# A two-layer decoder trunk: another order of the attention steps, and the embedding product among the output projection's last row blocks

## The chip, the core and the metric

The kernel runs on one core of a Trainium2 chip. The metric is device time in microseconds (us), the median of several executions. The engines' names in the profile are PE (TensorE, matmuls) with PEld (its weight loads), DVE (VectorE), ACT (ScalarE), POOL (GpSimd) and SP (SyncE, which here only issues DMAs). PSUM, where matmuls accumulate, has eight banks of 128 x 512 numbers.

## The reference

One sequence of 512 tokens with 1024 features, all in float32. `h` is the residual stream.

```python
def reference(x, p, ...):
    h = x
    for i in range(2):
        xn = rmsnorm(h, norm_mix[i])
        if i == 0:
            h = h + mixer_a(xn, a_w_in[0], a_norm_v[0], a_w_s[0], a_b_s[0], a_w_out[0])
        else:
            h = h + mixer_b(xn, b_w_q[0], b_sinks[0], b_w_o[0], kblk, vblk)
        h = h + conv_ffn(rmsnorm(h, norm_ffn[i]), f_w_up[i], f_conv_w[i], f_conv_b[i], f_w_down[i])
        h = h + per_layer_embed(h, p[i], norm_ple[i], ple_w_in[i], ple_w_gate[i], ple_b_gate[i])
        if i == 0:
            kblk, vblk = shared_kv(h, norm_kv, w_kv)   # 128-key blocks: the one before, and its own
    return rmsnorm(h, norm_final)

def mixer_b(xn, w_q, sinks, w_o, kblk, vblk):        # 16 heads of 64 in 4 groups, one K/V head a group
    q = (xn @ w_q).reshape(B, nb, BLOCK, N_KV_HEADS, GQA_GROUP, HEAD_DIM)
    scores = einsum('bnikgd,bnjkd->bnkgij', q, kblk) * HEAD_DIM ** -0.5
    scores = scores - slopes * dist                  # ALiBi: slope 2 ** (-(head + 1) / 2)
    scores = where(valid, scores, -inf)              # 0 <= dist < 128
    m = maximum(max(scores), sink)
    e = exp(scores - m)
    probs = e / (sum(e) + exp(sink - m))
    return einsum('bnkgij,bnjkd->bnikgd', probs, vblk).reshape(B, S, 1024) @ w_o

def conv_ffn(xn, w_up, conv_w, conv_b, w_down):      # 2816 hidden features, twice
    c = conv3(xn @ w_up)
    g, u = split(c, 2)
    return (silu(g) * u) @ w_down

def per_layer_embed(h, p_i, g_norm, w_in, w_gate, b_gate):
    return (p_i @ w_in) * sigmoid(rmsnorm(h, g_norm) @ w_gate + b_gate)   # p_i: 512 x 256
```

## The kernel before, in words

**Products.** Every large product is made of three matmuls a tile: each operand is split into a high part (a rounded copy, written by ACT) and a low part (the rest, written by DVE), and high x high, high x low and low x high are added in PSUM (`mm3`, lines 184 to 192; `mm3t` with the operands turned). Features lie on partitions, tokens along the row, so most matmuls are 128 x 128 by 128 x 512. In this document a *block* is one `mm3` over one 128-row slice: three matmuls.

**Weights.** `plan` lists all weight loads in the order of use, in units of up to 128 x 1024. `load` (L133) issues a unit's DMA on SP's queue into one of the raw tiles r0 to r5; during the attention only r0 and r1 are in use, since r2 to r5 hold attention tiles. `pump` (L148) converts a unit: cast `wh` on ACT (L163), subtraction `wl` on DVE (L164), into one of four buffers, or into tiles of its own where the plan names them. The activations p of the embedding go through the same list; their converted tiles take the places m4 and m5 of a pool that the attention uses for `prs` and for the masked copies of the even steps.

**The attention of layer 1** (L671 to L839) has 16 steps, 4 groups of heads by 4 token blocks. A step's work goes through these functions:

- `scores` (L681): 8 matmuls into the two banks `sc`.
- `logits` (L694): on DVE a masked copy (L701, not for the first token block), scale plus ALiBi (L702) and the row minimum `low` (L707); POOL first copies the sink column (L699). For the first token block a second masked copy (L704) follows.
- `exps` (L711): four exponentials on ACT. `weights` (L718): reciprocal on DVE, multiplication of `prs` on POOL (L722).
- `turn` (L724): four PE transposes into the bank `tr`; `turned_hi` (L744, ACT) and `turned_lo` (L750, DVE) split the result, and two masked copies on POOL (L753, `pm`) are made of it.
- `mix` (L756): the value product, four matmuls (two for the first token block) into the bank `pv`, with the key block before as a difference.
- `low_rows` (L773, ACT), `outputs` (L785 DVE, L789 ACT, L790 POOL or, for the last two, DVE): the heads' outputs as high and low tiles `o2`.

`slopes` (L676) makes the ALiBi tile of a group with four POOL products, once a group. `project` makes the queries of the next group, one block at a time; `queries` (L594) splits them (L252, L253) and moves their halves with four DMAs on SP's queue (L602, L603). `merge` makes parts of the output projection into a bank `mm` and adds the sum to `h` on DVE (L669). The loop at L811 runs a software pipeline: in iteration i scores(i), the value product of step i-2, logits(i), one or two of the other blocks, the turning of step i-1, then the rest of the blocks. Between them the iterations carry 6, 5, 5, 5, 5, 5, 5, 4, 4, 4 blocks of queries and then 4, 8, 4, 4, 8, 4 blocks of the first half of the projection. The first half of each row block m is closed and added to `h`; the second half follows in two further iterations and in the loop at L842, where `nf.take(m)` (L285) splits the finished row block for the next norm (ACT L248, DVE L249, square on ACT L277, sum on POOL L282).

**After it** comes the feed-forward part of layer 1 (`ffn`, L346): 22 up products `up(j)` of 16 blocks each, in three parts, each followed by its share of the down product (`dense_add`, L334). Just before the last share stands the layer's embedding product (`ple_in_both`, L407): for half of the tokens with features on partitions (48 matmuls of 256 columns), for the other half with tokens on partitions (24 matmuls of 512 columns), copied out of PSUM by ACT.

**Order.** The framework makes the semaphores, and it arranges each engine's queue by the written order and by what it reckons to be ready; so the trace follows the written order in the main, with some matmuls pulled ahead (in step 1, eleven matmuls of queries stand before the turning where six are written).

Of the kernel before, what the change touches and what calls it, by code (L numbers as in the profile page):

```python
# [52 lines left out]
def tile_yoco(ctx: ExitStack, tc: tile.TileContext, t, out: bass.AP, out_b: bass.AP):  # L53
# [40 lines left out]

    def plan_ffn(l):
        for i, (j0, j1) in enumerate(PARTS):
            if i == 0:
                plan_cols(t["w_up"][l], j1, KD)
            else:
                plan_cols(t["w_up"][l, j0 + 1 : j1], j1 - j0 - 1, KD)  # L100
            if i + 1 < len(PARTS):
                plan_cols(t["w_up"][l, j1 : j1 + 1], 1, KD)
            else:
                plan(t["pT"][l].rearrange("p a b -> p (a b)"), 2 * S, S, own=[(mp, "m4", "m5")])
                plan_cols(t["w_pin"][l], 2, 4)
            plan_cols(t["w_down"][l], 4, j1 - j0, k0=j0)
# [14 lines left out]
    for k0 in (0, 4):  # L121
        plan_cols(t["w_o"], 4, 4, k0=k0)
# [8 lines left out]
    state = {"raw": 0, "unit": 0, "next": 0, "tags": list(range(RAWS)), "turn": 0}  # L131
# [16 lines left out]
    def pump(upto):  # L148
        while state["unit"] < min(upto, len(units)):
# [184 lines left out]
    def dense_add(xs, kk, norm):  # L334

        for c in range(4):
            parts = chunk(256, kk)
            for j in range(2):
                m = 2 * c + j
                ps = psum(f"d{m}")  # L340
                mm3(ps, parts, xs, j * P)
# [4 lines left out]
    def ffn(l, norm, nxt):  # L346
# [35 lines left out]
        for i, (j0, j1) in enumerate(PARTS):  # L382
            act += [up(j) for j in range(j0 + 1, j1)]
            last = j1 == NJ
            if last:
                pe = ple_in_both() if l else ple_in(l)
            nact = [] if last else [up(j1)]
            dense_add(act, j1 - j0, nxt if last else None)
# [18 lines left out]
    def ple_in_both():  # L407

        pw = chunk(S, 2)
        px = [(a[:, o : o + S], b[:, o : o + S]) for a, b, o in pw]  # L410
        first = [(a[:, :N], b[:, :N]) for a, b in px]
        feat, tok = [], []
        for c in range(2):
            parts = chunk(256, 4)
            pf = mp.tile([P, 4, N], F32, tag=f"m{c}", name=f"pef{c}")
            for j in range(4):
                ps = psum(f"pinf{c}_{j}")[:, :N]
                mm3(ps, parts[j // 2 * 2 : j // 2 * 2 + 2], first, j % 2 * P)
                nc.scalar.copy(pf[:, j, :], ps)
                feat.append(pf[:, j, :])  # L420

            wh, wl = (x.rearrange("p (q k n) -> p q k n", q=2, k=2) for x in parts[0][:2])
            for i in range(2):
                if c == 0:
                    tok.append(mp.tile([P, D], F32, tag=f"m{2 + i}", name=f"pet{i}"))
                ps = psum(f"pint{c}_{i}")
                s = slice(N + i * P, N + (i + 1) * P)
                for k, (xh, xl) in enumerate(px):
                    nc.tensor.matmul(ps, xh[:, s], wh[:, :, k, :], start=k == 0, stop=False)
                    nc.tensor.matmul(ps, xl[:, s], wh[:, :, k, :], start=False, stop=False)  # L430
                    nc.tensor.matmul(ps, xh[:, s], wl[:, :, k, :], start=False, stop=k == 1)
                nc.scalar.copy(tok[i][:, c * S : (c + 1) * S], ps)
        return feat, tok
# [226 lines left out]
    def merge(m, k0, k1, first, last, tag="mm"):  # L660
# [4 lines left out]
        if first:  # L665
            box[f"o{m}"] = psum(f"o{m}_{half}", tag)
# [9 lines left out]
    def slopes(g):  # L676

        for e in range(GQ):
            nc.gpsimd.tensor_scalar_mul(alibi[:, e, :], dist, slope(GQ * g + e))
# [13 lines left out]

    def logits(i, o):  # L694
# [4 lines left out]
        nc.gpsimd.tensor_copy(pr[:, :, P], nsink[:, GQ * g : GQ * (g + 1)])  # L699
# [76 lines left out]
    def outputs(i, ps, b):  # L776
# [10 lines left out]
        for a in range(2):  # L787
            oh, ol = o2[2 * g + a]
            nc.scalar.copy(oh[:, cols], of[:, a, :])  # L789
            (nc.gpsimd if i < last - 1 else nc.vector).tensor_sub(ol[:, cols], of[:, a, :], oh[:, cols].bitcast(F32))  # L790

    last = len(steps)
    beside = {i: [] for i in range(last + 2)}
    u = 0
    for i, n in enumerate((6, 5, 5, 5, 5, 5, 5, 4, 4, 4)):
        beside[i] = [(project, u + a) for a in range(n)]
        u += n
    assert u == 48
    for a, ms in enumerate(((0,), (1, 2), (3,), (4,), (5, 6), (7,))):
        beside[10 + a] = [(merge, m, 0, 4, True, True) for m in ms]  # L800
    beside[16] = [(merge, m, 4, 6, True, False) for m in (0, 1)]
    beside[17] = [(merge, 2, 4, 6, True, False), (merge, 3, 4, 6, True, False), (merge, 4, 4, 6, True, False, "tr")]

# [5 lines left out]
    slopes(0)  # L809
    pump(state["next"] + WBUFS)  # L810
    for i in range(last + 2):  # L811
        if i < last:
            o = scores(i)
        if i >= 2:
            pv = mix(i - 2)
        if i < last:
            logits(i, o)
        if i >= 2:
            pb = low_rows(i - 2, pv)
        early = 2 if i < 10 else 1  # L820
        fill(i, 0, early)
        if 0 <= i - 1 < last:
            tr = turn(i - 1)
        if i >= 2:
            outputs(i - 2, pv, pb)
        if i < last:
            exps(i, (0,))
        if 0 <= i - 1 < last:
            turned_hi(i - 1, tr)
        if i < last:  # L830
            exps(i, (1, 2, 3))
        if 0 <= i - 1 < last:
            turned_lo(i - 1, tr)
        fill(i, early, None)
# [215 lines left out]
```

## Time and profile before

| | |
|---|---|
| median of 3 executions | 1153.9 us (1153.18 to 1155.84) |
| the profiled execution | 1154.12 us, of which span 1152.4 us |
| PE busy in the span | 1130.3 us |
| DVE, ACT, POOL busy | 737.9, 508.8, 148.6 us |
| mean granted clock of PE | 0.994 |
| attention steps in the trace | 594 to 698 us |
| last row blocks of the output projection | 698 to 716 us |
| embedding product of layer 1 | 1043 to 1054 us |

The times of the trace count from the start of the span. "Busy" of PE is drawn from modelled ends of pipelined matmuls: one 128 x 512 matmul shows 389 ns, while the next one starts 227 to 230 ns after it. A row of the groups of instructions reads: line, engine, operation, tile written and tiles read, shape, count, then busy us, mean ns of one, and the idle time of the engine before them with what ended it. A row of the waits reads: who waited, for whom, total us, how often, the longest.

### The profile page before, as it was taken

To read this page: it belongs to the slowest core of one execution; us is meant where nothing else is said; L and a number is where in the kernel's file an instruction comes from. 1 tells how busy PE (TensorE), PEld (TensorE's weight loads), DVE (VectorE), ACT (ScalarE), POOL (GpSimd) and SP (SyncE) were. 2 spreads that over 40 slices of the span, in tenths; PEclk is the share of its full clock that TensorE was granted. 3 is DMA by queue.
4 is the path that set the end of the run, shared out by engine and by line. 5 is a ranking of instruction groups with operands and counts; after the bars stand their busy time and mean duration, and the time that the engine had idled before them with its cause. 6 is when DMAs were issued, how large, how long until landed. Compare 5 with 4: busy or idle time off the path is not lost.

```text
span 1152.4 us, 13748 instructions
## 1 busy us (share of the span) xinstructions
PE 1130.3 (98%) x5248; PEld 938.4 (81%) x5248; DVE 737.9 (64%) x984; ACT 508.8 (44%) x811; POOL 148.6 (13%) x181
## 2 busy tenths in 40 slices
PE   9999999999999999999999999999999999999996
PEld 7888888888888888888888777788888888888895
DVE  7356477763676367557868787777636763675656
ACT  6534344431344234544567665444323442445542
POOL 2100310000000000022216654100000000000232
PEclk9999999999999999999999999899999999999998
DMA  9322322332322333232063323323323323333201
GB/s 328 103 89 86 98 94 92 108 98 85 110 83 82 110 122 95 78 114 104 19 175 102 108 74 111 108 78 106 104 80 109 85 81 113 119 100 112 87 18 73
DMA packets 44690, 116.48 MB, mean 101 GB/s; under 512 B 4936, under 2 KB 16848, under 8 KB 44624
## 3 DMA queue, kind: packets, MB, share of 16 engines
q1 hardware_dynamic: 43504, 114.42, 31.4%
q10 hardware_dynamic: 1120, 1.18, 0.3%
q8 instruction: 41, 0.67, 0.2%
q14 instruction: 25, 0.20, 0.1%
HBM read 108.24 MB, written 2.11 MB: 96 GB/s over the span
## 4 chain that ended last, share of the span: by engine, by line
PE 88%; DVE 4%; ACT 3%; POOL 2%; issue 1%; DMA 1%; SPq 0%; POOLq 0%; ACTq 0%; DVEq 0%
PE up L190 14%; PE up L191 14%; PE up L192 14%; PE d L190 8%; PE d L192 8%; PE d L191 8%; PE gate L190 2%; PE gate L192 2%; PE gate L191 2%; PE u L192 1%; PE u L190 1%; PE u L191 1%; PE v L202 1%; PE v L203 1%; PE v L201 1%
## 5 line engine op out<-in xcount | busy, mean ns | idle before, releaser
L164 DVE TENSOR_TENSOR wl<-wraw,wh 128x1024 fp32r<-128x1024 f32 (+2 forms) x197 | 237.9, 1209 | 126.2 <-ACT wh L163 123.6
L163 ACT CAST wh<-wraw 128x1024 fp32r<-128x1024 f32 (+1 forms) x196 | 202.2, 1032 | 239.5 <-PE d L191 133.1
L191 PE MATMUL up<-nf10l,wh 128*128 128x512 f32 x352 | 138.4, 393 | 1.0 <-DVE nf10l L249 1.0
L190 PE MATMUL up<-nf10h,wh 128*128 128x512 f32 x352 | 138.1, 392 | 0.6 <-ACT nf10h L248 0.6
L192 PE MATMUL up<-nf10h,wl 128*128 128x512 f32 x352 | 137.9, 392 | 0.0
L190 PE MATMUL up<-nf00h,wh 128*128 128x512 f32 x352 | 137.1, 390 | 0.0
L192 PE MATMUL up<-nf00h,wl 128*128 128x512 f32 x352 | 137.0, 389 | 0.0
L190 PE MATMUL d<-ah,wh 128*128 128x512 f32 x352 | 136.9, 389 | 0.0
L191 PE MATMUL up<-nf00l,wh 128*128 128x512 f32 x352 | 136.9, 389 | 0.0
L191 PE MATMUL d<-al,wh 128*128 128x512 f32 x352 | 136.9, 389 | 0.0
L192 PE MATMUL d<-ah,wl 128*128 128x512 f32 x352 | 136.9, 389 | 0.0
L368 ACT ACTIVATE c<-hs,vec 128x512 f32<-128x512 f32 x88 | 71.7, 815 | 88.2 <-DVE hs L364 87.5
L369 DVE SCALAR_TENSOR_TENSOR c<-hs,vec,c 128x511 f32<-128x511 f32 x88 | 65.8, 748 | 37.6 <-ACT c L368 37.4
L342 DVE TENSOR_TENSOR h<-h,d 128x512 f32<-128x512 f32 x56 | 38.4, 686 | 73.0 <-PE d L192 73.0
L191 PEld LDWEIGHTS up<-nf10l,wh 128*128 128x128 f32 x352 | 66.7, 190 | 15.4 <-DVE nf10l L249 1.7
L190 PEld LDWEIGHTS up<-nf10h,wh 128*128 128x128 f32 x352 | 66.7, 189 | 14.9 <-ACT nf10h L248 1.1
L192 PEld LDWEIGHTS up<-nf10h,wl 128*128 128x128 f32 x352 | 66.8, 190 | 14.0
L192 PEld LDWEIGHTS up<-nf00h,wl 128*128 128x128 f32 x352 | 66.1, 188 | 13.9
L192 PEld LDWEIGHTS d<-ah,wl 128*128 128x128 f32 x352 | 66.1, 188 | 13.8
L191 PEld LDWEIGHTS d<-al,wh 128*128 128x128 f32 x352 | 66.1, 188 | 13.7
L190 PEld LDWEIGHTS d<-ah,wh 128*128 128x128 f32 x352 | 66.1, 188 | 13.6
L190 PEld LDWEIGHTS up<-nf00h,wh 128*128 128x128 f32 x352 | 66.1, 188 | 13.6
(312 smaller groups left out, 2006.8 us busy)
## 6 DMA issues: line engine op xcount, KB each, us to landing
wraw<-in_w_up SPq DMA_DIRECT2D x88, 512.0 KB, 3.5
wraw<-in_w_down SPq DMA_DIRECT2D x32, 512.0 KB, 3.5
wraw<-in_w_down SPq DMA_DIRECT2D x16, 384.0 KB, 3.2
wraw<-in_w_u SPq DMA_DIRECT2D x8, 512.0 KB, 5.5
wraw<-in_w_out SPq DMA_DIRECT2D x8, 512.0 KB, 3.6
wraw<-in_w_gate SPq DMA_DIRECT2D x8, 512.0 KB, 3.7
wraw<-in_w_q SPq DMA_DIRECT2D x8, 512.0 KB, 4.0
wraw<-in_w_o SPq DMA_DIRECT2D x8, 512.0 KB, 3.3
```

What stands on the lines that cost most here:

```text
L163: nc.scalar.copy(wh[:, :n], src)
L164: nc.vector.tensor_sub(wl[:, :n], src, wh[:, :n].bitcast(F32))
L190: nc.tensor.matmul(ps, wh[:, a:b], xh, start=st, stop=False)
L191: nc.tensor.matmul(ps, wh[:, a:b], xl, start=False, stop=False)
L192: nc.tensor.matmul(ps, wl[:, a:b], xh, start=False, stop=en)
L201: nc.tensor.matmul(ps, xh[:, s], wh[:, a:b], start=st, stop=False)
L202: nc.tensor.matmul(ps, xl[:, s], wh[:, a:b], start=False, stop=False)
L203: nc.tensor.matmul(ps, xh[:, s], wl[:, a:b], start=False, stop=en)
L342: nc.vector.tensor_add(h[m], h[m], ps)
L368: nc.scalar.activation(c, hs, AF.Identity, bias=v("conv_b", l * 2 * NJ + col), scale=cw[2])
L369: nc.vector.scalar_tensor_tensor(c[:, 1:], hs[:, : S - 1], cw[1], c[:, 1:], op0=ALU.mult, op1=ALU.add)
```

## The change

Four parts.

1. *Order of a step.* In iteration i: scores(i), logits(i), weight conversion, three blocks, the turning of step i-1, a block, the value product of step i-2, a block. The exponentials, splits and outputs are written between them. The last steps are written out behind the loop. The sink column of the next step is copied at the end of a step, and the ALiBi tile of the next group is made by one DVE scaling in place, in the group's last step.
2. *Blocks.* 48 blocks of queries and 32 of the projection's first half form one list of 80, five to a step. The projection's row blocks 4 to 7 come first and are closed after their first half; row blocks 0 to 3 stay open in the four `mm` banks until their second half.
3. *Embedding product.* It is cut into eight pieces of about 1.4 us of matmuls, and one piece stands ahead of each of the last eight row blocks of the projection. Its loads move in the plan with it; a cap keeps their conversion behind the attention.
4. *Down product.* In the last share of layer 1, the first two row blocks run all but their last slice first, and then the last slice of both.

```diff
+    def plan_pin(l):
+        plan(t["pT"][l].rearrange("p a b -> p (a b)"), 2 * S, S, own=[(mp, "m4", "m5")])
+        plan_cols(t["w_pin"][l], 2, 4)
...
-    for k0 in (0, 4):
-        plan_cols(t["w_o"], 4, 4, k0=k0)
+    for c0, k0 in ((2, 0), (0, 0), (0, 4)):
+        plan_cols(t["w_o"][c0 : c0 + 2], 2, 4, k0=k0)
+    plan_cols(t["w_o"][2:3], 1, 4, k0=4)
+    held_back = len(units)
+    plan_pin(1)
+    plan_cols(t["w_o"][3:4], 1, 4, k0=4)
     plan_ffn(1)
...
+            if fresh and c == 0:
+                pss = [psum(f"d{j}") for j in range(2)]
+                for k0, k1 in ((0, kk - 1), (kk - 1, kk)):
+                    for j in range(2):
+                        mm3(pss[j], parts[k0:k1], xs[k0:k1], j * P, first=k0 == 0, last=k1 == kk)
...
+        def piece(u, ps):
+            c, q = u // 4, u % 4
+            if q == 0:
+                parts[c] = chunk(256, 4, ahead=2)
+                feat.append(mp.tile([P, 4, N], F32, tag=f"m{c}", name=f"pef{c}"))
+            if q < 2:
+                for j in range(2):
+                    mm3(ps[:, j * N : (j + 1) * N], parts[c][2 * q : 2 * q + 2], first, j * P)
+                nc.scalar.copy(feat[c][:, 2 * q : 2 * q + 2, :], ps.rearrange("p (j n) -> p j n", j=2))
+                return
...
-        nc.gpsimd.tensor_copy(pr[:, :, P], nsink[:, GQ * g : GQ * (g + 1)])
...
+        if n == NC - 1 and g + 1 < GROUPS:
+            nc.vector.tensor_scalar_mul(alibi, alibi, slope(GQ - 1))
...
+    work = [(project, u) for u in range(48)]
+    part = lambda m, k: (merge, m, k, k + 1, k == 0, k == 3 and m > 3)
+    work += [part(m, k) for m, k in ((4, 0), (4, 1), (5, 0), (5, 1), (4, 2), (4, 3), (5, 2), (5, 3))]
+    work += [part(m, k) for m in (6, 7, 0, 1, 2, 3) for k in range(4)]
+    beside = [work[5 * i : 5 * i + 5] for i in range(last)]
+    beside.append([(merge, m, 4, 6, False, False) for m in (0, 1)])
...
+    for i in range(last):
+        o = scores(i)
+        logits(i, o)
+        pump(state["next"] + WBUFS - 1)
+        fill(i, 0, 3)
+        if i:
+            tr = turn(i - 1)
+        exps(i, (0,))
+        if i:
+            turned_hi(i - 1, tr)
+        exps(i, (1,))
+        fill(i, 3, 4)
         if i >= 2:
             pv = mix(i - 2)
             pb = low_rows(i - 2, pv)
+        exps(i, (2, 3))
+        if i:
+            turned_lo(i - 1, tr)
         if i >= 2:
             outputs(i - 2, pv, pb)
+        fill(i, 4, None)
+        weights(i)
+        if i + 1 < last:
+            sinks(i + 1)
+    fill(last, 0, 2)
+    tr = turn(last - 1)
+    turned_hi(last - 1, tr)
+    turned_lo(last - 1, tr)
+    pv = mix(last - 2)
+    outputs(last - 2, pv, low_rows(last - 2, pv))
+    state["cap"] = len(units)
+    load(held_back + 2)
+    for m in (2, 3):
+        merge(m, 4, 6, False, False)
+    pv = mix(last - 1)
+    outputs(last - 1, pv, low_rows(last - 1, pv))
+    state["tags"], state["turn"] = list(range(RAWS)), 2
+    load(held_back + 6)
+    two = psum2("o5")
+    merge(4, 4, 6, True, False, psum("o4_1", "tr"))
+    merge(5, 4, 6, True, False, two[:, 0])
+    piece, pef, pet = ple_in_both()
     nf = Norm("nf1", [(xp, "x", gain("norm_ffn", 1))])
     for m in range(KD):
+        piece(m, two[:, 1] if m == 0 else psum(f"pin{m}", "pv" if m == 1 else "mm"))
-        if m < 5:
+        if m < 6:
             merge(m, 6, 8, False, True)
         else:
             merge(m, 4, 8, True, True)
         nf.take(m)
```

More of the change, by code (lines that the diff above doesn't have):

```diff
@@ L148, in pump @@
     def pump(upto):
[L149 removed]
+        while state["unit"] < min(upto, state["cap"]):
             u = state["unit"]
@@ L407, in ple_in_both @@
     def ple_in_both():
-        pw = chunk(S, 2)
+        pw = chunk(S, 2, ahead=0)
         px = [(a[:, o : o + S], b[:, o : o + S]) for a, b, o in pw]
         first = [(a[:, :N], b[:, :N]) for a, b in px]
[L412 to L432, printed above, removed]
@@ L692, in scores, with sinks @@
         return o
+    def sinks(i):
+        g = steps[i][0]
+        nc.gpsimd.tensor_copy(prs[:, i % 2, :, P], nsink[:, GQ * g : GQ * (g + 1)])
     def logits(i, o):
```

87 lines of the change are left out of this document (34 added, 53 removed).

## The prediction

> **What bounds the kernel now.** I read the page first, for the engine that is always busy.
>
> ```profile
> span 1152.4 us, 13748 instructions
> PE 1130.3 (98%) x5248; PEld 938.4 (81%) x5248; DVE 737.9 (64%) x984; ACT 508.8 (44%) x811; POOL 148.6 (13%) x181
> ```
>
> TensorE is the bound, and the change removes none of its work. So only its holes are to be won: waits, and stretches at a lowered clock, of which the page's clock row shows one in the middle, just behind the attention. The second view is busy time by stretch: the attention with the output projection, two stretches around that drop, and the embedding product where it stands now.
>
> ```profile
> 594.00:698.00 104.00, 98.56 (x507) 78.80 (x507) 81.16 (x138) 66.22 (x212) 60.90 (x97) 1.00 0.33 97
> ...
> 719.80:723.20 3.40, 1.89 (x6) 0.69 (x5) 3.40 (x5) 1.25 (x2) 0.50 (x1) 1.00 0.48 154
> 723.20:730.00 6.80, 6.49 (x16) 4.74 (x17) 2.92 (x6) 0.00 (x0) 2.93 (x1) 0.50 0.21 77
> 1043.00:1054.30 11.30, 11.30 (x74) 10.17 (x74) 5.71 (x7) 7.51 (x16) 0.00 (x0) 1.00 0.43 127
> ```
>
> Columns: stretch, length, then busy time of PE, PEld, DVE, ACT and POOL, then the clock. TensorE idles 5.4 us in the attention; from 719.8 to 723.2 it issues six matmuls while VectorE is busy without a break; then 6.8 us run at half clock. The third view, the waits of PE, names who it waits for (total, times, longest), from 594 to 698:
>
> ```profile
> PE pv L767 <- POOL pm L753: 2.7, 5, 0.8
> PE tr L729 <- POOL prs L722: 2.3, 3, 1.3
> PE pv L767 <- ACT pp L744: 0.2, 1, 0.2
> ```
>
> and from 698 to 731:
>
> ```profile
> PE up L191 <- DVE nf10l L249: 1.0, 2, 0.6
> PE up L190 <- ACT nf10h L248: 0.6, 1, 0.6
> PE nf1ms L296 <- DVE nf1fold L316: 0.2, 1, 0.2
> ```
>
> In the attention the value product (pv) waits for GpSimd's masked copies (pm), and the turning (tr) for GpSimd's weights (prs); behind it the first up product waits for the split of h. The chain of waits gives what a group costs TensorE when nothing holds it, and what a wait costs beyond its idle time:
>
> ```profile
> 622.80 0.95 PE sc L691 x8
> 623.75 0.92 PE pv L767 x4
> ...
> 626.06 0.44 PE tr L729 x4
> 626.50 0.23 PE q L190
> ...
> 697.24 0.04 issue
> 697.28 0.50 PE pv L767
> ```
>
> A matmul costs 0.23 us, a block (three) 0.69; the matmul behind a wait shows 0.50, so each wait costs another 0.27.
>
> **Part 1: value product later behind its turning.** In the steps of five blocks, turn(i-1) is now followed by three blocks, scores(i+1) and then the value product: 3 x 0.69 + 0.95 = 3.02 us of cover, by the written order, which the queues follow but for matmuls that are pulled ahead. After the change come a block, the older value product, a block, scores, three blocks, the next turning and a block: 6 x 0.69 + 0.92 + 0.95 + 0.44 = 6.45 us. What must fit in, with the rest of the step's work (lines view, attention):
>
> ```profile
> L715 ACT ACTIVATE prs<-prs,low 128x129 f32<-128x129 f32 x64 | 25.3, 398 | 8.5 <-DVE low L707 8.5
> ...
> L722 POOL TENSOR_TENSOR prs<-prs,sm 128x512 f32<-128x512 f32 x16 | 18.8, 1174 | 1.3 <-DVE sm L721 0.8 <-PE pv L767 0.4
> ...
> L753 POOL TENSOR_SCALAR_AFFINE_SELECT pm<-pp 128x512 fp32r<-128x512 f32 x16 | 12.8, 800 | 15.5 <-ACT pp L744 14.8 <-DVE pp L750 0.8
> ...
> L702 DVE SCALAR_TENSOR_TENSOR prs<-sc,rq,alibi 128x512 f32<-128x512 f32 x16 | 11.9, 747 | 1.4 <-POOL prs L699 0.3 <-POOL pm L753 0.2
> L707 DVE TENSOR_REDUCE low<-prs 128x4 f32<-128x516 f32 x16 | 10.8, 673 | 0.0
> ...
> L701 DVE COPY_PREDICATED sc<-above,sc 128x512 f32<-128x512 uint32 x12 | 8.2, 686 | 2.6 <-PE sc L691 2.5
> ...
> L679 POOL TENSOR_SCALAR alibi<-dist 128x128 f32<-128x128 f32 x12 | 6.3, 530 | 0.7 <-DVE prs L702 0.2
> ...
> L750 DVE TENSOR_TENSOR pl<-tr,ph 128x512 fp32r<-128x512 f32 x8 | 5.5, 689 | 3.4 <-ACT ph L744 3.3
> ...
> L744 ACT CAST ph<-tr 128x512 fp32r<-128x512 f32 x8 | 4.7, 587 | 3.8 <-PE tr L729 3.7
> ```
>
> Cast 0.59, subtraction 0.69 and a masked copy 0.80 follow one another: 2.1 us, with handovers (0.04 in the chain) and a POOL multiplication of 1.17 in the way some 3.4. That is why 3.02 just fails, five times by at most 0.8, and 6.45 has 3 us to spare. I take the pm and pp waits as gone: 2.9 us idle and 6 x 0.27 = 1.6 behind them, **4.5**. Bounds: 0 (they reappear elsewhere, rival 2) and 4.5.
>
> **Part 2: the weights' way to the turning.** From the end of scores(i) to turn(i) the cover was 0.92 + 5 x 0.69 + 0.44 + 0.95 + 0.92 + 2 x 0.69 = 8.06 us and becomes 3 blocks, tr, block, pv, block, scores, 3 blocks: 8 x 0.69 + 0.44 + 0.92 + 0.95 = 7.83. The way through it is 0.69 + 0.75 + 0.67 on DVE, 4 x 0.40 on ACT with the cast of 0.59 among them, and 1.17 on POOL: 5.5 us, some 6 with handovers, if no queue holds it up. Two holdups go: the sink columns are copied a step earlier, and 12 POOL products (6.3 us, row L679) become three VectorE products. A DVE scaling of twice that size is the nearest price:
>
> ```profile
> L525 DVE TENSOR_SCALAR zv<-zv,vrt x4: 748/748/754, 55.7 to 57.7; 128x1024 f32<-128x1024 f32 x4
> ```
>
> (the zv line's own view: min/median/max in ns), and of the weights in the last step the timeline has
>
> ```profile
> 691.59 2.09 POOL L722 TENSOR_TENSOR prs<-prs,sm 128x512 f32<-128x512 f32 x1
> ```
>
> Half of 748 is 0.37 us, three times in front of low: 0.4 to 1.1 us on that way, inside the 1.8 us of slack, so 0. The weight conversions are now written ahead of the exponentials: ACT has 2.1 us of waiting for DVE there. Of the turning's 2.3 us of waits 1.3 stand in the last step, where the weights took 2.09 us. There the cover was two value products, six blocks and a turning, 1.84 + 4.14 + 0.44 = 6.4; it becomes nine blocks, a turning and a value product, 7.6. I take 1.1 + 0.3 = **1.4** as gained and leave the other 1.0 where it is. Bounds: 2.3 + 3 x 0.27 = 3.1 gained, or the loss of rival 1.
>
> **Part 3: five blocks to a step.** The query rows of group 1 end with block 16, now the first of step 3 instead of the last of step 2, and scores(4) reads them through DMAs:
>
> ```profile
> L253 DVE TENSOR_TENSOR ql<-q,qh 128x512 fp32r<-128x512 f32 x6 | 4.1, 686 | 0.8 <-ACT qh L252 0.8
> ```
>
> and of the queue's issues, their ns and the time to landing,
>
> ```profile
> L603 SPq DMA_DIRECT2D q<-ql x16: 461/570/1425, 583.8 to 655.8; - x16
> ...
> DMA to landing us min/median/max: 2.2/2.4/3.2
> ```
>
> Cast 0.59 (as of ph), subtraction 0.69 (behind low, so 1 us later), four issues on SP's queue at some 0.57 of which two lie behind the subtraction, landing 2.4: 0.6 + 1.0 + 0.7 + 0.6 + 2.4 = 5.3 us. Cover: four blocks, tr, pv = 4.12, and 0.5 until the later heads are read: 4.6. Cost **0.7** once, between 0 and 2.5 (a landing of 3.2 behind a load on the queue). Groups 2 and 3 have over a step. Keeping four row blocks open in PSUM saves four additions of h on DVE, nothing on PE's path: 0.
>
> **Part 4: the embedding product moved.** The 48 + 24 matmuls take 11.3 us in either place (the windows row at 1043). With them move three loads on SP's queue, three casts (ACT), three subtractions (DVE) and the copies out of PSUM (eight of 512 columns on ACT instead of eight of 256 and four of 512); nothing on POOL. The third load's slot comes free latest, with the last value product. Until it is read PE has four blocks and four times a piece (11.3 / 8 = 1.4) and two row blocks' matmuls (1.4), 14 us, and a load needs
>
> ```profile
> wraw<-in_w_o SPq DMA_DIRECT2D x8, 512.0 KB, 3.3
> ```
>
> 3.3, a cast and a subtraction (1.46 below) behind it: hidden. p's own cast now waits on ACT for the last turning, whose tile it takes over. Behind it on ACT stand only copies that come after that turning themselves, and PE reads p two value products and 24 matmuls later (7.4 us): 0, unless it slips ahead of the last step's cast of ph, which costs a cast of p's size once, some 1 us.
>
> At the new place (lines view, 698 to 731):
>
> ```profile
> L190 PE MATMUL o<-oh,wh 128*128 128x512 f32 x27 | 10.5, 389 | 0.0
> ...
> L249 DVE SCALAR_TENSOR_TENSOR nf10l<-h,vec,nf10h 128x512 fp32r<-128x512 f32 x8 | 9.9, 1242 | 0.1
> ...
> L164 DVE TENSOR_TENSOR wl<-wraw,wh 128x1024 fp32r<-128x1024 f32 x4 | 5.9, 1464 | 0.0
> ...
> L669 DVE TENSOR_TENSOR h<-h,o 128x512 f32<-128x512 f32 x8 | 5.3, 678 | 3.1 <-PE o L192 3.1
> ```
>
> Now DVE is the slow one: adds, splits and four conversions are 21.1 us against 3 x 27 matmuls (18.6 us), so PE runs out of splits at 720. After the change PE has, from the last turning on, two value products 1.8, 84 matmuls of projection 19.3 and the pieces 11.3: 32.4 us. DVE has 5.3 + 9.9, five conversions 7.3, and some 3.5 for the last two steps: 26. The last split then ends 0.7 + 0.7 + 1.2 = 2.6 us behind the last matmul, under 21 up matmuls (4.8). What was lost: from 719.8 to 730.0, 10.2 us, 22 matmuls ran, worth 5.1. I take 0.5 as left, **4.6** gained; bounds 0 and 5.1.
>
> Of this 3.4 us is the half clock (6.8 x 0.5). In the rows it follows a stretch that was 1.89 of 3.40 us busy, and no single wait there is over 0.6 us; I take it that the thin stretch brought it on. The Trainium skill (TensorE: Matmul & The Clock Gate, Why this matters for your kernels) puts the drop to half clock down to idle gaps of more than some 3 us. By that rule these waits are no cause, filling them cures nothing, and the sum would be 3.4 us higher; this trace shows a drop without such a gap.
>
> At the old place the embedding covered the last activation, which ends at
>
> ```profile
> 1048.04 0.69 DVE L253 TENSOR_TENSOR al<-a,ah 128x512 fp32r<-128x512 f32 x1 [0.69 <-ACT ah L252]
> ```
>
> 1048.7, 5.7 us behind the last up matmul (1043.0). The new order of the first two down rows puts 36 matmuls ahead of it, 8.3 us: cost 0. If conversions of down weights slip between (0.96 to 1.23 each), it reaches 1.5 at most.
>
> **Sum.** 4.5 + 1.4 - 0.7 + 4.6 = 9.8 off. The profiled execution took 1154.1 (span 1152.4 and 1.7 around it), 0.2 above the median 1153.9; I forecast 1154.1 - 9.8 = 1144.3, against the median some 1144.2.
>
> **Rivals.** 1 (slower): the way from scores to weights becomes the bound of each step. For it: that cover is the only one that shrinks, and POOL holds weights, four masked copies or outputs in one queue; and in the last step it took 6.4 of cover and 1.3 of wait, 7.7. Against: two holdups leave it. A way of C us costs (C - 7.83)/2 a step, since each span holds two such waits; over 16 steps it eats the other gains (9.8 + 1.0 left in the sum) from C = 9.2. At 9.7 it costs 15.0: 1154.1 - 9.8 - 1.0 + 15.0 = 1158.
> 2: the attention's waits only change place (weights instead of masked copies, POOL being 60.9 of 104 us busy): parts 1 and 2 give nothing, 1144.3 + 5.9 = 1150.
> 3: DVE still holds the row blocks, with splits at 1.8 instead of 1.24 beside POOL's additions: 8 x 0.55 + 5 x 0.3 = 6 more fills the 32 us, part 4 gives nothing: 1149.
> 4: the clock drops all the same, after another thin stretch of some 3.4 us or for a cause that the rows don't show: 1144.3 + 3.4 = 1147.7. The clock page's rule, for which these waits are too short, would end here.
>
> **Numbers.** Forecast 0.47; rival 1 0.10, rival 2 0.19, rival 3 0.10, rival 4 0.10; no difference 0.04. Within 0.2% (2.3 us) is about what these runs cannot tell from nothing. Faster 0.86, same 0.04, slower 0.10. All holes closed would be 2.9 + 2.3 + 9 x 0.27 + 5.1 = 12.7 off, 1141.4: the low end is 1141. The high end, 1152, takes in rivals 2 to 4 with 2 us of part 3 and leaves out rival 1 and part of no difference.
>
> **What will show it.** Part 1: the row pv <- pm falls from 2.7 to under 0.5. Part 2: tr <- prs stays at 1 to 1.5; above 4, rival 1 is on its way. Part 3: a wait of sc for a q DMA near step 4. Part 4: no half clock before the end of the program, DVE under 85% busy from the last turning to the first up product, and no PE gap around the last down product. Wrong makes it above all a wait of the turning in nearly every step.

## The result, and the profile after

| | before | after |
|---|---|---|
| median of four executions each | 1154.01 us (1153.18 to 1155.84) | 1146.81 us (1146.44 to 1147.44) |
| ratio | | 0.9936, 95% interval 0.9919 to 0.9953 |
| profiled execution, its span | 1154.12, 1152.4 | 1146.59, 1144.9 |
| mean granted clock of PE | 0.994 | 0.997 |

The change takes off 7.2 us where 9.8 was forecast; the interval of the ratio is 5.4 to 9.3 us. A second set of runs of the same two kernels, beside the last experiments, gave 0.9942 (0.9928 to 0.9956).

First the page of the changed kernel, its span and its row of busy times:

```profile
span 1144.9 us, 13730 instructions
...
PE 1123.8 (98%) x5248; PEld 936.6 (82%) x5248; DVE 737.1 (64%) x983; ACT 509.7 (45%) x807; POOL 139.8 (12%) x169
```

TensorE is the bound as before, with the same 5248 matmuls. Next, busy time by stretch of the changed kernel (columns as in the prediction): the attention, the row blocks with the embedding pieces among them, and the first up products.

```profile
594.00:698.00 104.00, 98.00 (x510) 80.32 (x510) 82.77 (x138) 68.42 (x211) 52.67 (x85) 1.00 0.35 99
698.00:731.00 33.00, 33.00 (x169) 27.76 (x168) 23.00 (x28) 20.61 (x33) 8.53 (x7) 1.00 0.56 176
731.00:745.00 14.00, 14.00 (x63) 11.62 (x64) 8.38 (x12) 5.54 (x7) 2.94 (x1) 1.00 0.26 83
```

Behind the attention the hole is closed: PE is busy all 33 us, VectorE 23.00 of them (70%), and the clock stays at 1.00. In the attention PE idles 6.0 us (104 less 98.00), against 5.4 before. The waits of PE there, same kernel, 594 to 698 (from 698 to 731 that view is empty):

```profile
PE tr L750 <- POOL prs L743: 3.7, 6, 1.1
PE sc L707 <- DMA q<-ql: 1.6, 1, 1.6
PE o L198 <- POOL ol L813: 0.4, 1, 0.4
PE pv L788 <- DVE pb L806: 0.2, 1, 0.2
```

The five waits for masked copies and the one for pp (2.9 us) are gone. The turning waits six times instead of three, 3.7 us instead of 2.3, and the scores wait once, 1.6 us, for the query halves. In sum 5.9 us of waits, where it was 5.2.

Idle time doesn't count what a wait costs beyond it, so I also added up, over all matmuls of a stretch, the time to the next start less what that form takes when nothing holds it (0.23 us for 512 columns, 0.12 for 256, 0.11 for 128). This is my working from the trace, good to a few tenths since some records are missing:

| time lost by PE, us | before | changed | changed, embedding at its old place (experiment below) |
|---|---|---|---|
| 594 to 698, attention | 10.0 | 8.6 | 7.4 |
| 698 to 731, row blocks | 5.6 | 0.0 | 6.7 |
| sum | 15.6 | 8.6 | 14.1 |

So 5.6 of the 7.0 us come from behind the attention, and 1.4 from the attention itself, for which 5.2 (4.5 + 1.4 - 0.7) had been forecast.

This holds for the profile above. The changed kernel was profiled a second time, in the second set of runs, and that trace differs in one place. Around step 4 the turning waits 0.8 us and, right behind it, the scores wait 2.2 us for the query halves (0.8 and 1.6 in the first trace), and then the clock drops inside the attention. The stretch and the one behind it in the second trace, then the same stretch in the first:

```profile
617.00:620.40 3.40, 0.88 (x4) 0.27 (x2) 0.08 (x1) 0.46 (x2) 1.96 (x4) 1.00 0.25 69
620.40:627.20 6.80, 6.34 (x20) 5.41 (x21) 4.07 (x7) 2.69 (x8) 1.27 (x2) 0.50 0.20 48
```

```profile
617.00:620.40 3.40, 1.00 (x6) 0.43 (x4) 0.00 (x0) 0.32 (x2) 1.87 (x3) 1.00 0.59 169
```

The 6.8 us at half clock cost 3.4 us, and this execution took 1149.84 us, 3.5 above the median of its set (1146.39). By the mean clock on record for each execution the drop comes only in some: of the changed kernel's ten, two stand at 0.995 (1147.83 and 1149.84 us) and eight at 0.996 to 0.997 (1145.19 to 1147.44), and those of the kernel before run from 0.994 to 0.997 (1151.05 to 1156.46). So the change closed the hole behind the attention, but in two of the twelve traces with the new order (this one, and the one with the weights first below) the clock drops behind the new wait for the query halves.

### The profile page after: what moved, and what is told of

The parts are those of the page before. It is cut to its first block, busy times and chain, and to the rows that moved or that the text cites. A ratio compares the mean times of both kernels' runs of the same rounds, so it can differ in the third digit from the quotient of the medians.

```text
span 1144.9 us, 13730 instructions
## 1 busy us (share of the span) xinstructions
PE 1123.8 (98%) x5248; PEld 936.6 (82%) x5248; DVE 737.1 (64%) x983; ACT 509.7 (45%) x807; POOL 139.8 (12%) x169
## 4 chain that ended last, share of the span: by engine, by line
PE 89%; DVE 4%; ACT 2%; issue 2%; POOL 1%; DMA 1%; SPq 0%; POOLq 0%; ACTq 0%; DVEq 0%
PE up L197 14%; PE up L198 14%; PE up L199 14%; PE d L197 8%; PE d L199 8%; PE d L198 8%; PE gate L197 2%; PE gate L199 2%; PE gate L198 2%; PE u L199 1%; PE u L197 1%; PE u L198 1%; PE v L209 1%; PE v L208 1%; PE v L210 1%
## 5 line engine op out<-in xcount | busy, mean ns | idle before, releaser
L259 ACT CAST ah<-a 128x512 fp32r<-128x512 f32 x44 | 27.4, 622 | 113.5 <-DVE a L390 113.5
L198 PEld LDWEIGHTS up<-nf00l,wh 128*128 128x128 f32 x352 | 66.1, 188 | 13.6
```

The lines of the kernel that those rows point to most:

```text
L198: nc.tensor.matmul(ps, wh[:, a:b], xl, start=False, stop=False)
L259: nc.scalar.copy(hi, src)
```

## The experiments

All ratios are to the kernel before on the same chip. Fences with waits are those of PE from 590 to 735.

**The embedding put back.** The loads of the embedding, its product and the order of the down product are as before; the attention keeps its new order.

```diff
-            elif l == 0:
+            else:
                 plan_pin(l)
...
-    plan_pin(1)
...
-                pe = ple_in(l)
+                pe = ple_in_both() if l else ple_in(l)
...
-        piece(m, two[:, 1] if m == 0 else psum(f"pin{m}", "pv" if m == 1 else "mm"))
```

> The embedding product, its loads and its place ahead of the last down product go back to where they were before (the first two down rows in plain order again); the attention's new order stays. Theory A (part 4 of the prediction: the pieces cover the slow splits of h, and the half clock came from the thin stretch): PE waits again for nf1 splits, 1.5 to 2.5 us, a stretch of 6.8 us at half clock comes back behind the attention, and the time is 4.5 to 6 us above the changed kernel, about 1152. Rival (the half clock had to do with the attention's waits before it, which this kernel lacks): waits of about 2 us return without the half clock, about 1149. Rival 2 (the embedding's place is worth nothing): 1147.

Measured: 1152.31 us, ratio 0.9995 (0.9985 to 1.0004). The attention's new order alone can't be told from no change. The waits and the stretches behind the attention in this run:

```profile
PE tr L747 <- POOL prs L740: 3.6, 6, 1.1
PE up L197 <- DVE nf10l L255: 1.9, 2, 1.3
PE up L196 <- ACT nf10h L254: 0.6, 1, 0.6
PE sc L704 <- DMA q<-ql: 0.5, 1, 0.5
...
```

```profile
716.00:722.20 6.20, 3.73 (x14) 2.24 (x14) 6.20 (x7) 3.07 (x5) 2.10 (x2) 1.00 0.24 85
722.20:729.00 6.80, 6.40 (x16) 4.64 (x16) 2.61 (x5) 0.28 (x1) 2.93 (x1) 0.50 0.23 77
```

What follows: the masked copies' waits are gone here too, and 2.6 us of lost time are won in the attention (10.0 to 7.4; the changed kernel's 8.6 holds 1.1 us more of the scores' wait for the queries, 1.6 against 0.5). But 1.1 of them are given back behind it: VectorE, busy 6.20 of 6.20 us, holds the first up product longer than before (waits of 2.5 us instead of 1.6), and the half clock is as long as ever, 6.8 us. Moving the embedding is worth the difference between this ratio and the changed kernel's: 0.9995 - 0.9936 = 0.59%, 6.8 us by the medians and 5.5 by the lost time (14.1 - 8.6).

**Filling the thin stretch of the kernel before.** In the first up product, its last three blocks of one half are each followed by four matmuls whose sums are overwritten: 12 added matmuls, 2.8 us of work.

```diff
+            both = [psum(f"up{j}_{s}") for s in range(2)] if l and j == 0 else []
...
+                    for k in range(KD):
+                        mm3(ps, parts[k : k + 1], xs[k : k + 1], 0, first=k == 0, last=k == KD - 1)
+                        if k >= 5:
+                            for _ in range(4):
+                                nc.tensor.matmul(both[1], parts[0][0][:, :P], xs[0][0], start=True, stop=True)
```

> The kernel before, with twelve matmuls more: four behind the sixth, seventh and eighth slice of the first up product of layer 1, where PE waited 1.8 us for the splits of h. They write a bank that the next product starts afresh, so nothing that is computed changes. Theory A (the thin stretch of 3.4 us, 1.89 us busy, brought the half clock on): PE is over 80% busy there, the 6.8 us at half clock do not come, and the time falls by 3.4 less what the added matmuls cost beyond the waits (2.8 - 1.8 = 1.0), some 2.4 us: about 1151 where before is 1153.3. Rival (the drop has another cause, no wait there being longer than 0.6 us): the half clock stays, and the time is the same or 1 to 2 us longer.

Measured: 1151.62 us, ratio 0.9983 (0.9974 to 0.9991): faster by 2.0 us (1.0 to 3.0) with more work. The stretches and the one wait left there:

```profile
719.00:722.40 3.40, 3.40 (x17) 2.82 (x16) 3.40 (x4) 1.66 (x3) 1.36 (x1) 1.00 0.42 154
722.40:730.00 7.60, 7.26 (x34) 5.66 (x33) 3.87 (x7) 0.52 (x2) 2.94 (x1) 1.00 0.19 69
```

```profile
...
PE up L191 <- DVE nf10l L249: 0.3, 1, 0.3
...
```

The same wait for VectorE, now covered by matmuls, and the clock stays at 1.00. It is shown that at this place the thin stretch brought the half clock on: once it is filled, with matmuls whose sums nothing uses, the drop doesn't come.

**The down product in its plain order.** `fresh=False` in the changed kernel, nothing else.

> One change undone: the first two rows of the last down product of layer 1 run in plain order again, each with its last slice at its own end; the embedding product stays at its new place. Theory A (the new order is what covers the last activation, whose low part ended 5.7 us behind the last up matmul): 18 matmuls, 4.1 us, stand ahead of the first use, PE waits for al some 1.6 us, and the time is 1.3 to 2 us above the changed kernel. Rival (matmuls that are pulled ahead cover it anyway): no such wait, same time.

Measured: 1146.46 us, 0.9937 (0.9923 to 0.9951), as the changed kernel. At the last down product PE had no gap above 0.06 us. The framework's order pulls matmuls ahead there by itself. By the starts of the matmuls some 0.3 us are lost at 1050.6, which the changed kernel doesn't lose; the written order is worth that at most, too little for the times to show.

**Six blocks to the first step.** Blocks 6, 5, ..., 5, 4 instead of 5 each.

```diff
-    beside = [work[5 * i : 5 * i + 5] for i in range(last)]
+    cuts = [0] + [5 * i + 6 for i in range(9)] + [5 * i + 50 for i in range(7)]
+    beside = [work[a:b] for a, b in zip(cuts, cuts[1:])]
```

> One change: the first nine steps take their blocks one earlier (6 blocks in step 0, 5 in the others, 4 in step 9), so that the queries of group 1 are complete in step 2 and not with the first block of step 3. Theory A (the late block alone makes scores(4) wait 1.6 us for a query DMA): the wait of sc goes, and the time falls by the 1.6 us and its restart, 1.6 to 1.9 us, to about 1145. Rival (the wait comes from the weight load that stands ahead of the last two query DMAs on SP's queue, wherever the block is): the DMAs still land 4.6 us after their issue, and a wait of over 0.5 us stays; 1146 to 1147.

Measured: 1145.25 us, 0.9932 (0.992 to 0.9945).

```profile
PE tr L750 <- POOL prs L743: 2.5, 4, 0.9
PE o L198 <- POOL ol L813: 0.9, 1, 0.9
PE sc L707 <- DVE prs L721: 0.9, 1, 0.9
PE sc L707 <- DMA q<-ql: 0.5, 1, 0.5
...
```

The wait for the queries falls from 1.6 to 0.5 and those of the turning from 3.7 to 2.5; a wait of the scores for VectorE's first sums appears (0.9), and that of the projection for `ol` grows from 0.4 to 0.9. The ratio lies 0.04 to 0.1% under the two of the changed kernel, inside the intervals.

**Loads and conversions asked for at the step's end.** `pump` moved from behind the logits to the end of the iteration, ahead of the weights.

```diff
-        pump(state["next"] + WBUFS - 1)
         fill(i, 0, 3)
...
         fill(i, 4, None)
+        pump(state["next"] + WBUFS - 1)
         weights(i)
```

> One change: the weight conversion is written at the end of a step, as before the change, and no longer ahead of the exponentials. Theory A (casts of 1.04 us between the exponentials, as in step 8, make the way from scores to weights longer than its cover): the waits of the turning fall from 3.7 to 1 to 2 us, the time by 1.5 to 2.5 us, about 1145. Rival (the conversions only wait for their buffers, and the written place changes nothing): same waits, 1146.5 to 1147. The weight load that stood ahead of the query DMAs may also come later on SP's queue; then the wait of sc falls by up to 1.6 us besides.

Measured: 1146.64 us, 0.9943 (0.993 to 0.9955). The turning waits as in the changed kernel (3.7 us, six times). But the edit changed only the written place of the conversions: in step 8 of this run the cast still runs behind the first exponential (643.55) and ahead of the second, on ACT:

```profile
644.42 1.05 ACT L170 CAST wh<-wraw 128x1024 fp32r<-128x1024 f32 x1
645.37 0.40 ACT L736 ACTIVATE prs<-prs,low 128x129 f32<-128x129 f32 x1
```

So the written place is worth nothing, as the rival said, and what the cast costs at the place where it runs isn't tested. The wait for the queries is gone, though. SP's queue in the changed kernel, and the scores that wait:

```profile
612.33 2.28 SPq L620 DMA_DIRECT2D q<-qh  x2
614.71 0.53 SPq L151 DMA_DIRECT2D wraw<-in_w_o  x1
615.34 1.10 SPq L621 DMA_DIRECT2D q<-ql  x2
```

```profile
620.14 0.30 PE L707 MATMUL sc<-kh,q 128*128 128x128 f32 x1 [1.63 <-DMA q<-ql]
```

and SP's queue in this run:

```profile
612.58 1.10 SPq L620 DMA_DIRECT2D q<-qh  x2
613.78 0.53 SPq L151 DMA_DIRECT2D wraw<-in_w_o  x1
615.13 1.10 SPq L621 DMA_DIRECT2D q<-ql  x2
```

The weight load of 512 KB stands ahead of the two low halves (ql) in both. From issue to landing these two took, by each kernel's own view (min/median/max), first the changed kernel, then this run:

```profile
DMA to landing us min/median/max: 4.6/4.6/4.7
```

```profile
DMA to landing us min/median/max: 3.4/3.4/3.4
```

Over all their transfers of ql both have a median of 2.4. In the eleven profiles of the new order in which that load was issued up to 1.8 us ahead of them or 1.0 us behind, they took 3.3 to 5.7 us; in the run with four edits (below), where it came 1.4 us behind, 2.3, but in the kernel before, where it came 1.5 us behind, 3.1 to 3.2. That points to the load beside them, but no run takes it away, and the distance doesn't order the sizes: the changed kernel run again had the load 1.37 us ahead, as here (1.35), and they took 5.6 us and the scores waited 2.2. So that the wait is gone in this run isn't shown to be the edit's doing.

**The turning a block later.** Four blocks instead of three ahead of the turning.

```diff
-        fill(i, 0, 3)
+        fill(i, 0, 4)
...
-        fill(i, 3, 4)
+        fill(i, 4, 5)
...
-        fill(i, 4, None)
```

> One change: the turning stands behind four blocks of its step instead of three, the value product behind the fifth. The cover from scores to turning grows by one block, from 7.83 to 8.52 us; that from turning to value product stays at 6.45. Theory A (the six waits of the turning, 3.7 us, are a way from scores to weights that is longer than the cover by at most 1.1 us): they fall to 0.5 to 1.5 us, the time by 2 to 3.5 us, to 1143.5 to 1145. Rival (the way stretches with PE, since ACT and DVE take up work that the later turning and value product release later): the waits stay at 3 us or more, 1146 to 1147.

Measured: 1146.25 us, 0.9941 (0.9928 to 0.9953). The turning waits 2.8 us (five times, at most 0.8). A block more of cover took 0.9 us of waits off instead of nearly all, since the way from the scores to the weights grew along with it (from 7.9 to 8.6 us at the median, read as below).

**The scaling of the distances behind the row minimum.** The three VectorE scalings in place change places with `low`.

> One change: the scaling of the ALiBi tile (0.66 us on VectorE, three times) stands behind the row minimum of its step instead of ahead of it. Theory B (what makes the way from scores to weights longer than its cover is work that stands on VectorE's queue between the masked copy and the row minimum: this scaling, and weight conversions of 1.2 to 1.5 us): the turning's waits at steps 3 and 11, 0.8 and 0.4 us, shrink to under 0.3 each, the total from 3.7 to 2.5 to 3; the time falls by 0.8 to 1.3 us. Rival (POOL's queue holds the weights): the total stays at 3.5 or more.

Measured: 1146.45 us, 0.9938 (0.9924 to 0.9951). The scaling was taken as 0.37 us; it takes 0.66 (lines view of the changed kernel):

```profile
L726 DVE TENSOR_SCALAR alibi<-alibi 128x512 f32<-128x512 f32 x3 | 2.0, 657 | 0.0
```

Behind `low` it takes the waits of steps 3 and 11 from 0.77 and 0.37 to 0.25 and 0.14 us, in all from 3.7 to 2.8. On the time that isn't resolved.

**No low part of the weights inside the attention.** The subtraction is left out for the units converted in the steps, and the high part is read in its place.

```diff
+            if state.get("bare") and not own:
+                wl = wh
+            else:
```

> Left out: the subtraction that makes the low part of a weight unit, for the units converted during the attention steps; the matmuls that read the low part read the high part instead. VectorE loses some ten instructions of 1.2 to 1.5 us, every other engine keeps its work. Theory B (conversions on VectorE's queue lengthen the way from scores to weights): the turning's waits fall from 3.7 to under 1.5 us, the time by 2 to 3 us. Rival (casts on ACT between the exponentials, or POOL's queue): they stay at 3 us or more.

Measured: 1145.38 us, 0.9927 (0.9912 to 0.9942). Waits of the turning 2.9 us (four times, at most 1.0), of the scores 1.2. VectorE has nine instructions less than in the changed kernel (974 against 983 on the pages, 10.9 us of busy time), and three quarters of the waits are left. In step 14 of this run the follow-up of the value product stands in the way (VectorE's timeline):

```profile
683.39 0.85 DVE L809 TENSOR_TENSOR pb<-pv,pb 64x256 f32<-64x256 f32 x2 [0.69 <-ACT pb L797]
684.27 0.18 DVE L745 RECIPROCAL sm<-sm 128x4 f32<-128x4 f32 x1
```

The exponentials had ended at 683.8; the reciprocal stands behind additions that wait for ACT's copy of the value product, which part 1 has put later. That made the last theory, C.

**The weights written ahead of the value product's follow-up.**

```diff
         if i >= 2:
             pv = mix(i - 2)
-            pb = low_rows(i - 2, pv)
         exps(i, (2, 3))
         if i:
             turned_lo(i - 1, tr)
+        weights(i)
         if i >= 2:
-            outputs(i - 2, pv, pb)
+            outputs(i - 2, pv, low_rows(i - 2, pv))
         fill(i, 4, None)
-        weights(i)
```

Beside it ran the changed kernel again, this edit with the scaling behind `low` and `pump` at the end (three edits), and those with six blocks first (four edits).

> The changed kernel itself, on the chip of the three runs beside it, so that they can be compared with it there. Expected as it was: near 0.9936 of the kernel before, six waits of the turning for the weights, 3.7 us in all, and one of 1.6 us of the scores for the q transfer.

> The instructions of the weights of a step are written ahead of the follow-up of the value product (low rows and outputs), which are put behind them; nothing else differs. Theory C: the follow-up stands in the way from the scores to the weights on VectorE and ScalarE, because the value product now comes later; then the turning's waits fall from 3.7 us to under 1.5, and the time from about 1146.6 by 2 to 3 us to about 1144. Rival: the way is long by its own work and whichever other work the engines put into it; then the waits stay between 2.5 and 4 us and the time within 1 us of the changed kernel.

> As the run with the weights first, with two further edits that each took something away alone: the scaling of the distances behind the row minimum, and the loads and conversions asked for at the step's end. Theory C: no wait of the scores for the q transfer (it was 1.6 us), turning waits under 1 us, so about 3.5 us below the changed kernel, 1143. Rival (waits change place): other waits, of the scores for the first sums and of the output product for its low part, add up to over 1.5 us, and the time is above 1144.5.

> As the run with three edits, and the blocks six to the first step, then five, and four to the last. Alone it was worth about 1 us of waits. Theory C: 0 to 1 us below the run with three edits, about 1142.5. Rival: nothing beside the other three, within 0.5 us of it.

| | time, us | ratio, interval | waits of tr | of sc for q |
|---|---|---|---|---|
| changed kernel again | 1146.39 | 0.9942 (0.9928 to 0.9956) | 3.6, five | 2.2 |
| weights first | 1146.17 | 0.9939 (0.9927 to 0.9951) | 3.6, four | 1.2 |
| three edits | 1146.45 | 0.9943 (0.9930 to 0.9956) | 3.5, six | 0.9 |
| four edits | 1145.17 | 0.9931 (0.9920 to 0.9943) | 4.2, five | none |

Theory C missed: 3.6 us of waits where under 1.5 was expected, and no time won. The way itself did get shorter. From the end of a step's scores to the end of its weights (start and end of the rows of L707 and L743, step by step) the median of the 16 steps is 8.6 us before, 7.9 after and 7.3 with the weights first. What is left stands in four steps of 8.2 to 9.2 us. VectorE in one of them, step 14 of the run with the weights first, scores ended at 679.4:

```profile
680.74 0.68 DVE L720 COPY_PREDICATED sc<-above,sc 128x512 f32<-128x512 uint32 x1
681.52 0.75 DVE L721 SCALAR_TENSOR_TENSOR prs<-sc,rq,alibi 128x512 f32<-128x512 f32 x1
682.38 1.23 DVE L171 TENSOR_TENSOR wl<-wraw,wh 128x1024 fp32r<-128x1024 f32 x1
683.52 0.68 DVE L728 TENSOR_REDUCE low<-prs 128x4 f32<-128x516 f32 x1
684.12 0.68 DVE L771 TENSOR_TENSOR pp<-tr,pp 128x512 fp32r<-128x512 f32 x1
684.72 0.84 DVE L806 TENSOR_TENSOR pb<-pv,pb 64x256 f32<-64x256 f32 x2
685.49 0.68 DVE L720 COPY_PREDICATED sc<-above,sc 128x512 f32<-128x512 uint32 x1
686.19 0.18 DVE L742 RECIPROCAL sm<-sm 128x4 f32<-128x4 f32 x1
```

and PE behind it:

```profile
688.10 0.66 PE L750 MATMUL tr<-ident,prs 128*128 128x128 f32 x4 [1.18 <-POOL prs L743]
```

A weight conversion stands between the first sums and the row minimum, and a masked copy of the *next* step ahead of the reciprocal, although both are written elsewhere: the framework arranges the queue by what it reckons ready. In the twelve profiles with the new order, whichever holder an edit removed, the turning's waits summed to 2.5 to 4.2 us. Not tried: weights first without the conversions. So what would bring these waits to nothing stays open.

With four edits the ql transfers stand ahead of the load and the q wait is gone. It is, beside the one with six blocks first, the fastest kernel with all the work, but against the changed kernel's two ratios, 0.9936 and 0.9942, nothing is resolved.

## Why the prediction was right or wrong

The direction, the range and the size within 2.6 us came out, but with the parts in other proportions: the attention's 5.2 us were 1.4, and part 4's 4.6 were 5.6. That the sum came so near is in part luck: part 4's surplus of 1.0 covers some of the 3.8 that the attention fell short by, and the first profiled run met no clock drop in the attention.

*Part 1* said that 6.45 us of cover leave the masked copies' row under 0.5. They do: the row is gone. The bound "0 (they reappear elsewhere, rival 2)" is what the time shows, though: the cover works, and its gain is mostly taken by parts 2 and 3 and by what follows the attention.

*Part 2* is the term that failed: "the way through it is ... 5.5 us, some 6 with handovers, if no queue holds it up", hence "1.8 us of slack". The waits of tr were to fall to 1.0 and rose from 2.3 to 3.7: a term of +1.4 that should have been about -1.4 in idle time alone. The sum of durations was right as a sum, but queues hold the way up in every step: in the trace of before it already took 6.6 to 11.2 us, in the changed kernel 6.9 to 9.1, against a cover of 7.83. The holders can be read in step 8 of the changed kernel, on ACT:

```profile
645.00 0.41 ACT L736 ACTIVATE prs<-prs,low 128x129 f32<-128x129 f32 x1 [2.58 <-DVE low L728]
645.31 0.19 ACT L736 ACTIVATION_READ_ACCUMULATOR prs<-prs,low 128x1 f32 x1
645.40 0.56 ACT L765 CAST pp<-tr 128x512 fp32r<-128x512 f32 x1
645.87 1.04 ACT L170 CAST wh<-wraw 128x1024 fp32r<-128x1024 f32 x1
646.81 0.40 ACT L736 ACTIVATE prs<-prs,low 128x129 f32<-128x129 f32 x1
```

"ACT has 2.1 us of waiting for DVE there" counted a conversion's cast as free since it is written ahead of the exponentials; here it runs between two of them, although the row minimum had long been done. The 2.1 isn't in the rows either: that of the exponentials has 8.5 us of waiting for `low` in 16 steps, 0.5 a step. In this step ACT does wait 2.58 us, but the cast comes behind that wait and not in it. What the cast adds to the way wasn't measured by itself. The turning then waits:

```profile
650.62 0.66 PE L750 MATMUL tr<-ident,prs 128*128 128x128 f32 x4 [1.09 <-POOL prs L743]
```

It is the longest of the six waits. The scaling's price of 0.37 (measured 0.66) was a second, smaller miss of this part. Single edits take shares off (0.9 each for the block of cover and the scaling), none the whole, so part 2's cause is shown only in part.

*Part 3* named the place, "scores(4)", and the mechanism, a landing "behind a load on the queue". The size was off: 0.7 forecast, 1.6 measured (2.2 in the second set of runs), inside its bounds of 0 to 2.5, because the landing took 4.6 us and not 2.4 (at its bound 3.2). What no term of the sum held is the clock: in the second trace this wait and the turning's ahead of it were followed by 6.8 us at half clock, another 3.4 us.

*Part 4* was forecast at 4.6 and gave 5.6, with nothing left of what was lost: the 0.5 taken as left isn't there, and beside the new attention it has more to cover (6.7 us in the run with the embedding put back). VectorE is 70% busy there, under the 85% named as sign. The old place cost nothing, as said, and the new down order had no share in that.

*Rivals.* Rival 2, that the attention's waits only change place, is the nearest to what happened in the attention (0.9995 for its new order alone), while its 1150 was too slow because part 4 gave more than its term. Rival 1 didn't come about: waits in six steps, not each. Rival 3 fell. Rival 4 fell at the place that it was made for, behind the attention, and in the first trace altogether; in the second trace the clock drops all the same, in the attention, after another thin stretch of 3.4 us and at the 3.4 us that rival 4 named.

## What to carry to other kernels

The slack of a chain through several queues is read from the trace, step by step, as the time from its first cause to its last effect; the sum of its durations is only the lower end, and here it was 2.6 us too short at the median. Moving one wait's cover lets the next holder in the same queues show, so a written order should be judged by the trace of the order that the framework makes of it. Work that depends on little, as the embedding product here, can be placed where another engine is the bound: it filled the hole and kept the clock up there. A new wait should be priced with the clock, too: 2.2 us of waiting for a transfer were followed by a drop that cost 3.4 more.

## What the hardware showed

*The clock can halve after a thin stretch, without a long gap.* Before, 1.89 of 3.40 us busy and no wait above 0.62 us were followed by 6.8 us at 0.50; in the run with the embedding put back it was 3.73 of 6.20, no wait above 1.31, and again 6.8 us; in the second trace of the changed kernel 0.88 of 3.40, no wait above 2.21, and 6.8 us; with the weights first 1.53 of 3.40, no wait above 1.24, and 3.4 us:

```profile
617.10:620.50 3.40, 1.53 (x8) 0.80 (x6) 0.76 (x3) 1.09 (x3) 2.52 (x6) 1.00 0.39 110
620.50:623.90 3.40, 3.32 (x10) 2.87 (x11) 1.18 (x3) 0.59 (x1) 0.87 (x2) 0.50 0.00 0
```

With 12 filler matmuls it was 3.40 of 3.40, and no drop. The Trainium skill (TensorE: Matmul & The Clock Gate, Why this matters for your kernels) puts a drop in mid-kernel down to idle gaps of more than some 3 us; three of these four traces disagree with that, and in the fourth, the second of the changed kernel, two waits with one matmul between them add up to 3.0 us. A rule by the busy share alone doesn't fit either: the first trace of the changed kernel has 1.00 of 3.40 at 617.00 (above) and 1.62 of 3.40 near its end, both without a drop:

```profile
1096.70:1100.10 3.40, 1.62 (x15) 1.38 (x14) 2.10 (x5) 1.17 (x3) 1.72 (x5) 1.00 0.00 0
```

In the clock records of the traces every stretch at full clock that ends in a drop lasts a whole multiple of 3.4133 us (614.40 us are 180, 716.80 are 210, 1133.23 are 332), and a half clock in mid-program lasts one or two of them. In the four traces with a drop the thin stretch fills one such period, and at 617.00 in the first trace it lies across two. So its place against the period may count; that isn't tested, and the stretch at 1096.70, which fills one too, speaks against it. The rule stays open.

*A transfer of 128 KB close to a load of 512 KB took up to 2.4 times its usual time*: 3.3 to 5.7 us in eleven profiles, instead of a median of 2.4, with the same two instructions at the same distance giving 3.4 once and 5.6 another time. What sets the size within that, the runs don't show.

*The same instruction has another price in another order of the work.* GpSimd's masked copies of `pp` took 0.64 us a piece (0.80 before) and the multiplication of the weights 1.04 (1.17 before); what beside them makes the difference isn't shown. The lines view of the changed kernel:

```profile
L743 POOL TENSOR_TENSOR prs<-prs,sm 128x512 f32<-128x512 f32 x16 | 16.7, 1042 | 4.1 <-DVE sm L742 3.5
...
L774 POOL TENSOR_SCALAR_AFFINE_SELECT pm<-pp 128x512 fp32r<-128x512 f32 x16 | 10.2, 637 | 14.0 <-ACT pp L765 13.1 <-DVE pp L771 0.6
```
